# Gathered cumulative sum and matmul on one core: rows converted to fp16 by the gather's own transfer, with 32 slots paced by landings, in place of fp32 slots and a ScalarE cast

## The chip, the core and the metric

The kernel runs on one core of a Trainium2 chip. The metric is the device time of one execution in microseconds. A core has TensorE (PE, matmuls; its weight loads are shown apart as PEld), VectorE (DVE), ScalarE (ACT), GpSimd (POOL), SyncE (SP), and 16 DMA engines that all queues share. Each engine works through its own list of instructions in order; engines wait for one another by semaphores.

## The reference

```python
B, S, N, D = (16, 4096, 2048, 512)          # x: (B, S, D) float32, w: (D, D) float32
# indices: (B, N) int64, per batch N different rows out of S, sorted
gathered = x[b_idx, indices, :].copy()
cs = np.cumsum(gathered, axis=1)
return np.matmul(cs, w).astype(np.float32)   # (B, N, D)
```

For each of 16 batches, 2048 rows of 512 numbers are picked out, summed cumulatively along the rows, and multiplied by w.

## The kernel before

The work is cut into T = 256 tiles of P = 128 gathered rows, 16 tiles (NT) to a batch; two tiles (R) make a pair. A tile passes through these steps, each on one engine:

1. POOL, `gather` (L127, the transfer at L137): an indirect DMA brings 128 rows of x, 2 KB each, into half of a buffer `g32` (8 buffers of a pair, so NG = 16 slots of a tile, fp32). Each slot has a semaphore `s_g` that the landing raises. Before a pair is gathered into a used buffer, POOL waits (L130) until the casts that read it are done (`s_c`).
2. ACT, `cast` (L148, L152): waits for landings and copies `g32` into `g16` (8 buffers of a pair, fp16), a tile or a whole pair at once.
3. PE, `sums` (L156, L164): four matmuls of 128 columns multiply the tile with a triangle of ones (`ut`), which gives the running sums within the tile, transposed, in the PSUM buffer `pa` (4 of them). Its columns are ordered so that two adjacent output rows come to one partition. PE waits for the cast (L159), for a free `pa`, and for a free `pb` of the coming projection (L163).
4. DVE, `carry` (L173, L196): adds the last column of the tile before, and writes `cst` as fp16. The first tile of a batch is only copied (L183).
5. PE, `project` (L200, L208): four matmuls of 512 columns multiply by w (fp16) into the PSUM buffer `pb` (4 of them).
6. ACT, `drain` (L217, L220): copies `pb` into an output buffer `ob` (8 buffers of a pair, fp32).
7. SP, `store` (L222, L234): when a pair is drained, a DMA of 512 KB writes it out. The first and the last pair, which use the triangle `uq` with rows in plain order, are stored tile by tile (L229).

The order of the work is written out by hand for each engine. On PE, a list `order` puts the sums of up to `lead` tiles ahead of projection u: `lead` is 1 at the start, grows with u to LEAD = 4, and shrinks to 1 at the end. On ACT, step u first waits, at every second tile, for the buffer `ob` to be stored, then makes the casts of step u, then drains tile u. How far those casts reach is planned at L114 to L122: two tiles ahead of u at the start, one more for each four tiles, FAR = 10 at most, and fewer again at the end; from a reach of five on they are made in pairs. PE, DVE and ACT have the first and last tiles unrolled, and roll the middle in loops of 16 tiles (U).

At the start, indices of the first four tiles come through two small loads (`idx_first`), and POOL gathers those tiles at once; the others come through `idx64`, a conversion to fp32, a transpose on PE and a copy back to integers (`idxg`), for which the gather of tile 4 waits. w is loaded as fp32 and cast half by ACT and half by DVE.

Of the kernel before, what the change touches and what calls it, by code (L numbers as in the profile page):

```python
# [7 lines left out]
P = 128  # L8
FP32 = mybir.dt.float32
FP16 = mybir.dt.float16  # L10
# [23 lines left out]
def kernel(  # L34
# [7 lines left out]
    nc = tc.nc  # L42

    B, S, D = x.shape
    N = indices.shape[1]
    R = 2
# [3 lines left out]
    T = B * NT  # L50
    G = T // R
    GB = NT // R
    KI = T // P
    FIRST = 2 * R
    NG = 16
    LEAD = 4
    FAR = 10
    NH = 8
    NA = 4
    NB = 4  # L60
    NC = 4
    NO = 8
    U = NT
    assert U % NG == 0 and U % (R * NO) == 0 and U % NA == 0 and U % (R * NC) == 0 and U % NB == 0
    assert D == 512 and N % (R * P) == 0 and T % P == 0

    x_flat = x.rearrange("b s d -> (b s) d")
# [1 line left out]
    const = ctx.enter_context(tc.tile_pool(name="const", bufs=1))  # L69
# [10 lines left out]
    ident = const.tile([P, P], FP32)  # L80
    zeros = const.tile([P, D], FP16)
    spare = const.tile([P, 1], FP16)
    g32 = [const.tile([P, R, D], FP32, name=f"g32_{i}") for i in range(NG // R)]
    g16 = [const.tile([P, R, D], FP16, name=f"g16_{i}") for i in range(NH)]
    cst = [const.tile([P, DC, R, P], FP16, name=f"cst{i}") for i in range(NC)]
    ob = [const.tile([P, R, D], FP32, name=f"ob{i}") for i in range(NO)]
    pa = [ps.tile([P, DC, R, Q], FP32, name=f"pa{i}") for i in range(NA)]
    pb = [ps.tile([P, D], FP32, name=f"pb{i}") for i in range(NB)]

# [2 lines left out]
    def sem(name):  # L92
        return tc.alloc_semaphore(name)

    s_z, s_ut, s_wc, s_if, s_pt, s_prep, s_of, s_c = (
        sem(f"s_{n}") for n in ("z", "ut", "wc", "if", "pt", "prep", "of", "c")
    )
    s_first = [sem(f"s_first{k}") for k in range(2)]
    s_w = [sem(f"s_w{c}") for c in range(DC)]
    s_idx = [sem(f"s_idx{k}") for k in range(KI)]  # L100
    s_el = [sem(f"s_el{j}") for j in range(R)]
    s_ol = [sem(f"s_ol{j}") for j in range(R)]
    s_g = [sem(f"s_g{i}") for i in range(NG)]
    s_o = [sem(f"s_o{i}") for i in range(NO)]
    s_a = sem("s_a")
    s_d = sem("s_d")
    s_b = sem("s_b")
    s_e = sem("s_e")

    pool, pe, dve, act, sp = (  # L110
        Lane(e) for e in (nc.gpsimd, nc.tensor, nc.vector, nc.scalar, nc.sync)
    )

    casts = []  # L114
    cast_by = []
    for u in range(T):
        far = min(FAR, 2 + u // 4, 2 + (T - 1 - u) // 4)
        casts.append([])
        while len(cast_by) <= min(u + far, T - 1):
            n = R if far > 4 and len(cast_by) % R == 0 else 1  # L120
            casts[u].append((len(cast_by), n))
            cast_by += [cast_by[-1] + 1 if cast_by else 1] * n  # L122

    for u in range(3 * U, T - 2 * U):
        assert casts[u] == [(t + U, n) for t, n in casts[u - U]]

    def gather(t):  # L127
        g, r = divmod(t, R)
        if t >= NG:
            pool.need(s_c, cast_by[R * (g + 1) - NG - 1])  # L130
        if t < FIRST:
            pool.need(s_first[g], 16)
            ap = idx_first[:, t, 0:1]
        else:
            pool.need(s_prep, t // P + 1)
            ap = idxg[:, t // P, t % P : t % P + 1]
        nc.gpsimd.indirect_dma_start(  # L137
            out=g32[g % (NG // R)][:, r, :],
            out_offset=None,
            in_=x_flat,  # L140
            in_offset=bass.IndirectOffsetOnAxis(ap=ap, axis=0),
            element_offset=(t // NT) * S * D,
        ).then_inc(s_g[t % NG], 16)
# [1 line left out]

    PLAIN = (0, G - 1)

    def cast(t, n, first=None):  # L148
        g, r = divmod(t, R)
        for u in range(t, t + n):  # L150
            act.need(s_g[u % NG], 16 * (u // NG + 1), first)
        nc.scalar.copy(  # L152
            out=g16[g % NH][:, r : r + n], in_=g32[g % (NG // R)][:, r : r + n]
        ).then_inc(s_c, 1)

    def sums(t, u, first=None):  # L156
        g, r = divmod(t, R)
        tiles = None if first is None else R * first
        pe.need(s_c, cast_by[t] if first is None else cast_by[2 * U + t] - 2 * U // R, first)  # L159
        pe.need(s_d, t - NA + 1, tiles)  # L160
        for c in range(DC):
            if c == 1 and u is not None:
                pe.need(s_e, u - NB + 1, tiles)  # L163
            mm = nc.tensor.matmul(  # L164
                out=pa[t % NA][:, c],
                lhsT=g16[g % NH][:, r, c * P : (c + 1) * P],
                rhs=uq[:] if first is None and g in PLAIN else ut[:],
                start=(c == 0),
                stop=(c == DC - 1),
            )  # L170
        mm.then_inc(s_a, 1)
# [28 lines left out]
    def project(u, t, first=None):  # L200
        g, j = divmod(u, R)
        tiles = None if first is None else R * first
        pe.need(s_e, u - NB + 1, tiles)
        pe.need(s_d, u + 1 if first is None and g in PLAIN else R * (g + 1), tiles)
        for c in range(DC):
            if c == 2 and t is not None:
                pe.need(s_d, t - NA + 1, tiles)
            mm = nc.tensor.matmul(  # L208
                out=pb[u % NB][:],
                lhsT=cst[g % NC][:, c, j, :],  # L210
                rhs=w16[:, c, :],
                start=(c == 0),
                stop=(c == DC - 1),
            )
        mm.then_inc(s_b, 1)

    def drain(u, first=None):  # L217
        g, j = divmod(u, R)
        act.need(s_b, u + 1, first)
        nc.scalar.copy(out=ob[g % NO][:, j], in_=pb[u % NB][:]).then_inc(s_e, 1)  # L220

    def store(g):  # L222
        b, h = divmod(g, GB)
        rows = out[b, h * R * P : (h + 1) * R * P, :]
        if g in PLAIN:
            for j in range(R):
                sp.need(s_e, R * g + j + 1)
                done = s_ol[j] if g else (s_o[0], s_of)[j]
                nc.sync.dma_start(  # L229
                    out=rows[j * P : (j + 1) * P, :], in_=ob[g % NO][:, j]  # L230
                ).then_inc(done, 16)
            return
        sp.need(s_e, R * (g + 1))
        nc.sync.dma_start(  # L234
            out=rows.rearrange("(p j) d -> p j d", j=R), in_=ob[g % NO][:]
        ).then_inc(s_o[g % NO], 16)


    with nc.allow_non_contiguous_dma(reason="a few indices, one per partition"):
        for k, eng in enumerate((nc.sync, nc.scalar)):  # L240
            t = k * R
            eng.dma_start(
                out=idx_first[:, t : t + R, :],
                in_=indices[0, t * P : (t + R) * P]
# [4 lines left out]
    for k in range(KI):  # L249
        nc.sync.dma_start(  # L250
            out=idx64[:, k, :], in_=idx_rows[k * P : (k + 1) * P, :]
        ).then_inc(s_idx[k], 16)
    for c in range(DC):
        eng = (nc.sync, nc.scalar)[c % 2]
        eng.dma_start(out=w32[:, c, :], in_=w[c * P : (c + 1) * P, :]).then_inc(s_w[c], 16)
    for g in range(G):
        store(g)
    for g in range(G - NO, G - 1):
        sp.need(s_o[g % NO], 16 * (g // NO + 1))
    for j in range(R):  # L260
        sp.need(s_ol[j], 16)


    nc.gpsimd.memset(ident[:], 1.0).then_inc(s_ut, 1)
# [3 lines left out]
        out=ident[:],  # L268
        in_=ident[:],
# [7 lines left out]
        out=ut[:],  # L277
        in_=ut[:],
# [9 lines left out]
        out=uq[:],  # L288
        in_=uq[:],
# [6 lines left out]
    for t in range(T):  # L296
        gather(t)
# [15 lines left out]
    for k in range(KI):  # L313
# [3 lines left out]
            out=pb[k % NB][:, :P], in_=idxf[:, k, :], identity=ident[:]  # L317
# [20 lines left out]
    order = []  # L338
    done = 0
    for u in range(T):  # L340
        lead = min(LEAD, 1 + (u + 2) // 4, 1 + (T - 1 - u) // 6)
        first = u if u // R in PLAIN else u // R * R + R - 1
# [2 lines left out]
            done += 1  # L345
        order.append((False, u))

    head = order.index((False, 2 * U - 1)) + 1
    tail = order.index((False, T - 2 * U - 1)) + 1
    step = 2 * U  # L350
    for i in range(head + step, tail):
        assert order[i] == (order[i - step][0], order[i - step][1] + U)

    def run(i, first=None):
        is_sums, t = order[i]
        after = next((v for k, v in order[i + 1 :] if k != is_sums), None)
        if first is not None:
            t -= 2 * U
            after -= 2 * U
        if is_sums:  # L360
            sums(t, after, first)
        else:
            pe.need(s_wc, DC)
            project(t, after, first)

    for i in range(head):
        run(i)
    with nc.tensor.Fori(2 * U // R, (T - 2 * U) // R, U // R) as first:
        pe.new_pass()
        for i in range(head, head + step):  # L370
            run(i, first)
    for i in range(tail, len(order)):
        run(i)
# [5 lines left out]
        act.need(s_w[c], 16)  # L379
        nc.scalar.copy(out=w16[:, c, :], in_=w32[:, c, :]).then_inc(s_wc, 1)  # L380
    def step(u, first=None):
        if u % R == 0:
            if first is None and u == R * NO:
                act.need(s_of, 16)
            act.need(s_o[u // R % NO], 16 * (u // R // NO), first)
        for t, n in casts[u if first is None else 2 * U + u]:
            cast(t if first is None else t - 2 * U, n, first)
        drain(u, first)


    for u in range(2 * U):
        step(u)
# [36 lines left out]
```

## Time and profile before

| what | value |
|---|---|
| time, median of 4 runs (lowest to highest) | 353.01 us (352.86 to 354.24) |
| the profiled execution: its own time | 352.79 us |
| its span, first to last instruction | 351.1 us |
| mean TensorE clock granted | 0.985 |
| busy: PE, PEld, DVE, ACT, POOL | 306.1, 156.2, 179.2, 262.5, 244.4 us |
| moved by DMA | 135.69 MB, mean 386 GB/s |
| HBM read, written | 68.42 MB, 67.11 MB |
| issue to landing, median: gather, store of 512 KB, store of 256 KB | 10.1, 6.7, 3.8 us |

In the prediction, lines of costly groups read: line of the kernel, engine, operation, output from input, count; then busy time in total and mean ns of one; then the idle time of the engine just before these instructions and what ended most of it ("issue" is time in which the engine waited for nothing that the profile shows). A strip has 40 numbers, one for each equal slice of the span. A queue's line gives its packets, its megabytes and the time that its packets took as a share of the 16 DMA engines' span; q0 carries the gathers and q1 nearly all else. A line of the chain of waits has the start and the duration in us, the engine and the line of the kernel. Landing times give the shortest, the median and the longest from issue to landing.

### The profile page before, as it was taken

The page shows a single profiled execution, that of the slowest core. Times are in us where ns is not written, and L with a number is a line of the kernel's source. Part 1 is how long each engine was busy: PE and PEld are TensorE (multiplying, and loading weights), DVE is VectorE, ACT ScalarE, POOL GpSimd, SP SyncE. Part 2 cuts the span into 40 slices and gives each one's busy share as a digit, 9 for nine tenths or more (in the row PEclk, how much of TensorE's full clock was granted, in tenths as well). Part 3 has the DMA queues.
Part 4 walks back from the last instruction along what each step waited for, and adds up shares of the span by engine and source line. Part 5 has one row for each costly group of instructions (what it writes and reads, how often), then busy time and mean ns, then how long its engine had stood idle before and what let it go on. Part 6 is the DMA issues. An engine that isn't in the chain of part 4 may idle for free.

```text
span 351.1 us, 6498 instructions
## 1 busy us (share of the span) xinstructions
PE 306.1 (87%) x2066; PEld 156.2 (44%) x2066; DVE 179.2 (51%) x263; ACT 262.5 (75%) x399; POOL 244.4 (70%) x266
## 2 busy tenths in 40 slices
PE   7656799989998989989898988989898999899993
PEld 2323355444444444444444444445444444445541
DVE  2433356555555555545555554555555555556451
ACT  3555599687787878778787877777787877788872
POOL 6777777777777777777777777777777777776000
PEclk9998899999999999999999999999999999999998
DMA  7899999999999999999999999999999999999983
GB/s 232 245 331 315 300 350 411 414 411 416 413 415 414 416 416 414 416 414 414 414 414 414 413 412 409 410 413 411 414 409 404 413 408 413 412 411 412 418 338 140
DMA packets 40619, 135.69 MB, mean 386 GB/s; under 512 B 6816, under 2 KB 7072, under 8 KB 40608
## 3 DMA queue, kind: packets, MB, share of 16 engines
q0 software_dynamic: 20480, 67.13, 50.0%
q1 hardware_dynamic: 19568, 67.91, 48.0%
q10 hardware_dynamic: 560, 0.53, 0.4%
q8 instruction: 5, 0.08, 0.1%
q14 instruction: 6, 0.05, 0.0%
HBM read 68.42 MB, written 67.11 MB: 386 GB/s over the span
## 4 chain that ended last, share of the span: by engine, by line
POOL 43%; DMA 18%; issue 16%; PE 15%; ACT 6%; DVE 0%; ACTq 0%; SPq 0%
POOL g L137 43%; DMA g<-in_x_dram,idxg 16%; PE pb L208 11%; ACT g L152 4%; PE pa L164 3%; ACT ob L220 2%; DMA g<-in_x_dram,idx_first 1%; DMA idx_first<-in_indices_dram 1%; DVE cst L183 0%; DVE cst L196 0%; ACTq L26 0%; ACTq L393 0%; SPq L424 0%; SPq L90 0%
## 5 line engine op out<-in xcount | busy, mean ns | idle before, releaser
L137 POOL DMA_INDIRECT g<-in_x_dram,idxg x252 | 238.9, 948 | 76.8 <-issue 71.4
L208 PE MATMUL pb<-w,cst 128*128 128x512 f16 x1024 | 264.8, 382 | 1.0 <-DVE cst L196 0.8
L196 DVE TENSOR_TENSOR cst<-pa,cst 128x512 f16<-128x512 f32 x240 | 166.1, 692 | 144.8 <-PE pa L164 143.9
L152 ACT CAST g<-g 128x1024 f16<-128x1024 f32 (+1 forms) x139 | 135.9, 979 | 58.2 <-DMA g<-in_x_dram,idxg 57.3
L220 ACT COPY ob<-pb 128x512 f32<-128x512 f32 x256 | 138.5, 586 | 19.6 <-PE pb L208 19.5
L164 PE MATMUL pa<-ut,g 128*128 128x128 f16 x1008 | 113.7, 222 | 34.9 <-ACT ob L220 22.2
L164 PEld LDWEIGHTS pa<-ut,g 128*128 128x128 f16 x1008 | 73.4, 98 | 116.3 <-ACT ob L220 53.8
L208 PEld LDWEIGHTS pb<-w,cst 128*128 128x128 f16 x1024 | 90.1, 98 | 64.1 <-issue 2.6
L183 DVE CAST cst<-pa 128x512 f16<-128x512 f32 x16 | 11.1, 692 | 13.3 <-PE pa L164 13.3
L304 PE MATMUL pb<-zeros 128*128 128x512 f16 x16 | 5.7, 524 | 1.5 <-DVE zeros L308 1.5
L137 POOL DMA_INDIRECT g<-in_x_dram,idx_first x4 | 4.0, 997 | 1.6 <-issue 0.9
L304 PEld LDWEIGHTS pb<-zeros 128*128 128x128 f16 x16 | 2.0, 132 | 4.0 <-issue 1.9
L380 ACT CAST w<-w 128x512 f16<-128x512 f32 x2 | 1.1, 616 | 3.0 <-DMA w<-in_w_dram 3.0
L377 ACT ACT_TABLE_LOAD x1 | 1.3, 1283 | 2.5 <-issue 2.5
L164 PE MATMUL pa<-uq,g 128*128 128x128 f16 x16 | 1.6, 220 | 1.7 <-ACT g L152 1.7
L311 DVE CAST idxf<-idx 128x128 f32<-128x128 uint32 x2 | 0.5, 227 | 4.1 <-DMA idx<-in_indices_dram 4.1
L164 PEld LDWEIGHTS pa<-uq,g 128*128 128x128 f16 x16 | 1.0, 97 | 3.0 <-issue 1.7
L325 DVE CAST w<-w 128x512 f16<-128x512 f32 x2 | 0.8, 424 | 1.3 <-DMA w<-in_w_dram 1.3
L316 PE MATMUL pb<-ident,idxf 128*128 128x128 f32 x2 | 0.9, 448 | 0.3 <-DVE idxf L311 0.3
L316 PEld LDWEIGHTS pb<-ident,idxf 128*128 128x128 f32 x2 | 0.4, 182 | 1.2 <-DVE idxf L311 0.8
L308 DVE MEMSET zeros<- 128x256 uint32 x1 | 0.3, 272 | 1.1 <-SPq L90 1.1
L322 DVE CAST idxg<-pb 128x128 uint32<-128x128 f32 x2 | 0.6, 288 | 0.4 <-PE pb L316 0.4
(11 smaller groups left out, 2.1 us busy)
## 6 DMA issues: line engine op xcount, KB each, us to landing
out_dram<-ob SPq DMA_DIRECT2D x126, 512.0 KB, 6.7
g<-in_x_dram,idxg POOLq DMA_INDIRECT x252, 10.1
out_dram<-ob SPq DMA_DIRECT2D x4, 256.0 KB, 3.8
w<-in_w_dram ACTq DMA_DIRECT2D x2, 256.0 KB, 4.1
w<-in_w_dram SPq DMA_DIRECT2D x2, 256.0 KB, 4.8
idx<-in_indices_dram SPq DMA_DIRECT2D x2, 128.0 KB, 3.4
g<-in_x_dram,idx_first POOLq DMA_INDIRECT x4, 4.6
idx_first<-in_indices_dram ACTq DMA_DIRECT2D x1, 2.0 KB, 2.1
```

The lines of the kernel that those rows point to most:

```text
L137: nc.gpsimd.indirect_dma_start(out=g32[g % (NG // R)][:, r, :], out_offset=None, in_=x_flat, in_offset=bass.IndirectOffsetOnAxis(ap=ap, ax ...
L152: nc.scalar.copy(out=g16[g % NH][:, r : r + n], in_=g32[g % (NG // R)][:, r : r + n]).then_inc(s_c, 1)
L164: mm = nc.tensor.matmul(out=pa[t % NA][:, c], lhsT=g16[g % NH][:, r, c * P : (c + 1) * P], rhs=uq[:] if first is None and g in PLAIN else ...
L183: nc.vector.tensor_copy(out=dst, in_=src).then_inc(s_d, 1)
L196: nc.vector.tensor_tensor(out=dst, in0=src, in1=last, op=mybir.AluOpType.add).then_inc(s_d, 1)
L208: mm = nc.tensor.matmul(out=pb[u % NB][:], lhsT=cst[g % NC][:, c, j, :], rhs=w16[:, c, :], start=(c == 0), stop=(c == DC - 1),)
L220: nc.scalar.copy(out=ob[g % NO][:, j], in_=pb[u % NB][:]).then_inc(s_e, 1)
L304: nc.tensor.matmul(out=pb[NB - 1][:], lhsT=zeros[:, :P], rhs=zeros[:], start=True, stop=True)
L316: nc.tensor.transpose(out=pb[k % NB][:, :P], in_=idxf[:, k, :], identity=ident[:]).then_inc(s_pt, 1)
L325: nc.vector.tensor_copy(out=w16[:, c, :], in_=w32[:, c, :]).then_inc(s_wc, 1)
L377: nc.scalar.copy(out=spare[:], in_=zeros[:, :1])
L380: nc.scalar.copy(out=w16[:, c, :], in_=w32[:, c, :]).then_inc(s_wc, 1)
```

## The change

- The gather (L125 after the change) writes into fp16 buffers `g16` at once: 16 buffers of a pair, 32 slots of a tile (NG). The DMA converts fp32 to fp16 on its way. `g32` and ScalarE's cast, with its plan of casts, are removed.
- POOL's waits are others. Ahead of the first gather of a pair, it waits until the sums of the tiles that used the two slots before are done (`s_a`, the pair 32 tiles back). Ahead of the second, from tile 17 on, it waits for the landing of the gather 16 tiles before (FLY), so that at most 17 gathers are on their way.
- PE's sums wait for the landing (`s_g`) in place of the cast.
- Output buffers hold two pairs (W = 2) and there are four of them, as much room as before; a store of 1 MB writes two pairs. The first two pairs and the last two are stored singly, the very first and last still tile by tile. ACT waits for a free output buffer at every fourth tile.
- PE's loop has 32 tiles (V) in its body in place of 16. ACT's loop keeps 16 tiles and has drains and waits for output buffers alone.

Cut to its core:

```diff
-    NG = 16
+    NG = 32
+    FLY = 16
     LEAD = 4
-    FAR = 10
-    NH = 8
...
-    NO = 8
+    W = 2
+    NO = 4
     U = NT
+    V = 2 * U
...
-    g32 = [const.tile([P, R, D], FP32, name=f"g32_{i}") for i in range(NG // R)]
-    g16 = [const.tile([P, R, D], FP16, name=f"g16_{i}") for i in range(NH)]
+    g16 = [const.tile([P, R, D], FP16, name=f"g16_{i}") for i in range(NG // R)]
...
-    ob = [const.tile([P, R, D], FP32, name=f"ob{i}") for i in range(NO)]
+    ob = [const.tile([P, W, R, D], FP32, name=f"ob{i}") for i in range(NO)]
...
     def gather(t):
         g, r = divmod(t, R)
-        if t >= NG:
-            pool.need(s_c, cast_by[R * (g + 1) - NG - 1])
+        if r == 0:
+            pool.need(s_a, R * (g + 1) - NG)
+        elif t >= FLY:
+            pool.need(s_g[(t - FLY) % NG], 16 * ((t - FLY) // NG + 1))
...
         nc.gpsimd.indirect_dma_start(
-            out=g32[g % (NG // R)][:, r, :],
+            out=g16[g % (NG // R)][:, r, :],
...
-    def cast(t, n, first=None):
-        g, r = divmod(t, R)
-        for u in range(t, t + n):
-            act.need(s_g[u % NG], 16 * (u // NG + 1), first)
-        nc.scalar.copy(
-            out=g16[g % NH][:, r : r + n], in_=g32[g % (NG // R)][:, r : r + n]
-        ).then_inc(s_c, 1)
-
     def sums(t, u, first=None):
...
-        pe.need(s_c, cast_by[t] if first is None else cast_by[2 * U + t] - 2 * U // R, first)
+        pe.need(s_g[t % NG], 16 * (t // NG + 1), first)
...
-        nc.scalar.copy(out=ob[g % NO][:, j], in_=pb[u % NB][:]).then_inc(s_e, 1)
+        nc.scalar.copy(out=ob[g // W % NO][:, g % W, j], in_=pb[u % NB][:]).then_inc(s_e, 1)
...
-        sp.need(s_e, R * (g + 1))
+        sp.need(s_e, R * (g + n))
+        done = {1: s_of, G - W: s_ol}.get(g, s_o[g // W % NO])
         nc.sync.dma_start(
-            out=rows.rearrange("(p j) d -> p j d", j=R), in_=ob[g % NO][:]
-        ).then_inc(s_o[g % NO], 16)
+            out=rows.rearrange("(g p j) d -> p g j d", p=P, j=R),
+            in_=src[:, g % W : g % W + n],
+        ).then_inc(done, 16)
...
-    for g in range(G):
-        store(g)
...
+    for g in range(W):
+        store(g, 1)
+    for g in range(W, G - W, W):
+        store(g, W)
+    for g in range(G - W, G):
+        store(g, 1)
...
-    with nc.tensor.Fori(2 * U // R, (T - 2 * U) // R, U // R) as first:
+    with nc.tensor.Fori(V // R, (T - V) // R, V // R) as first:
...
     def step(u, first=None):
-        if u % R == 0:
-            if first is None and u == R * NO:
-                act.need(s_of, 16)
-            act.need(s_o[u // R % NO], 16 * (u // R // NO), first)
-        for t, n in casts[u if first is None else 2 * U + u]:
-            cast(t if first is None else t - 2 * U, n, first)
+        if u % (W * R) == 0:
+            if first is None and u == W * R * NO:
+                act.need(s_of, 16 * (R + W - 2))
+            act.need(s_o[u // R // W % NO], 16 * (u // R // W // NO), first)
         drain(u, first)
```

More of the change, by code (lines that the diff above doesn't have):

```diff
@@ L61 @@
     NC = 4
-    NO = 8
+    W = 2
+    NO = 4
     U = NT
-    assert U % NG == 0 and U % (R * NO) == 0 and U % NA == 0 and U % (R * NC) == 0 and U % NB == 0
+    V = 2 * U
+    assert V % NG == 0 and V // R == 16 and U % (W * R * NO) == 0 and U % NA == 0 and U % (R * NC) == 0 and U % NB == 0
     assert D == 512 and N % (R * P) == 0 and T % P == 0
@@ L100 @@
     s_idx = [sem(f"s_idx{k}") for k in range(KI)]
-    s_el = [sem(f"s_el{j}") for j in range(R)]
-    s_ol = [sem(f"s_ol{j}") for j in range(R)]
+    s_ol = sem("s_ol")
     s_g = [sem(f"s_g{i}") for i in range(NG)]
@@ L112 @@
     )
[L114 to L125, printed above, removed]
     def gather(t):
         g, r = divmod(t, R)
-        if t >= NG:
-            pool.need(s_c, cast_by[R * (g + 1) - NG - 1])
+        if r == 0:
+            pool.need(s_a, R * (g + 1) - NG)
+        elif t >= FLY:
+            pool.need(s_g[(t - FLY) % NG], 16 * ((t - FLY) // NG + 1))
         if t < FIRST:
@@ L165, in sums @@
                 out=pa[t % NA][:, c],
-                lhsT=g16[g % NH][:, r, c * P : (c + 1) * P],
+                lhsT=g16[g % (NG // R)][:, r, c * P : (c + 1) * P],
                 rhs=uq[:] if first is None and g in PLAIN else ut[:],
@@ L219, in drain, with store @@
         act.need(s_b, u + 1, first)
-        nc.scalar.copy(out=ob[g % NO][:, j], in_=pb[u % NB][:]).then_inc(s_e, 1)
-    def store(g):
+        nc.scalar.copy(out=ob[g // W % NO][:, g % W, j], in_=pb[u % NB][:]).then_inc(s_e, 1)
+    def store(g, n):
         b, h = divmod(g, GB)
-        rows = out[b, h * R * P : (h + 1) * R * P, :]
+        rows = out[b, h * R * P : (h + n) * R * P, :]
+        src = ob[g // W % NO]
         if g in PLAIN:
@@ L227, in store @@
                 sp.need(s_e, R * g + j + 1)
-                done = s_ol[j] if g else (s_o[0], s_of)[j]
+                done = s_ol if g else (s_o[0], s_of)[j]
                 nc.sync.dma_start(
-                    out=rows[j * P : (j + 1) * P, :], in_=ob[g % NO][:, j]
+                    out=rows[j * P : (j + 1) * P, :], in_=src[:, g % W, j]
                 ).then_inc(done, 16)
             return
-        sp.need(s_e, R * (g + 1))
+        sp.need(s_e, R * (g + n))
+        done = {1: s_of, G - W: s_ol}.get(g, s_o[g // W % NO])
         nc.sync.dma_start(
-            out=rows.rearrange("(p j) d -> p j d", j=R), in_=ob[g % NO][:]
-        ).then_inc(s_o[g % NO], 16)
+            out=rows.rearrange("(g p j) d -> p g j d", p=P, j=R),
+            in_=src[:, g % W : g % W + n],
+        ).then_inc(done, 16)
     with nc.allow_non_contiguous_dma(reason="a few indices, one per partition"):
@@ L255 @@
         eng.dma_start(out=w32[:, c, :], in_=w[c * P : (c + 1) * P, :]).then_inc(s_w[c], 16)
-    for g in range(G):
-        store(g)
[L258 to L261, printed above, removed]
+    for g in range(W):
[4 more added lines that the diff above has]
+        store(g, 1)
+    for i in range(G // W - NO, G // W - 1):
+        sp.need(s_o[i % NO], 16 * (i // NO + 1))
+    sp.need(s_ol, 16 * (R + W - 1))
     nc.gpsimd.memset(ident[:], 1.0).then_inc(s_ut, 1)
@@ L346 @@
         order.append((False, u))
-    head = order.index((False, 2 * U - 1)) + 1
-    tail = order.index((False, T - 2 * U - 1)) + 1
-    step = 2 * U
+    head = order.index((False, V - 1)) + 1
+    tail = order.index((False, T - V - 1)) + 1
+    step = 2 * V
     for i in range(head + step, tail):
-        assert order[i] == (order[i - step][0], order[i - step][1] + U)
+        assert order[i] == (order[i - step][0], order[i - step][1] + V)
     def run(i, first=None):
@@ L357, in run @@
         if first is not None:
-            t -= 2 * U
-            after -= 2 * U
+            t -= V
+            after -= V
         if is_sums:
```

## The prediction

> **What bounds the kernel now.** I read the page's costliest groups first, then the rate strip, the waits, and last the landings and the chain by stage.
>
> ```profile
> span 351.1 us, 6498 instructions
> L137 POOL DMA_INDIRECT g<-in_x_dram,idxg x252 | 238.9, 948 | 76.8 <-issue 71.4
> L208 PE MATMUL pb<-w,cst 128*128 128x512 f16 x1024 | 264.8, 382 | 1.0 <-DVE cst L196 0.8
> L152 ACT CAST g<-g 128x1024 f16<-128x1024 f32 (+1 forms) x139 | 135.9, 979 | 58.2 <-DMA g<-in_x_dram,idxg 57.3
> ```
>
> A gather keeps POOL 0.948 us and the next follows 0.30 us later, so one every 1.253 us. The timeline of POOL shows the first of these 252 at 8.39 us and the last at 322.89: 314.5/251 = 1.253. The gap is 0.30 both for gathers with no wait (tiles 4 to 15) and for those whose wait on a cast has been met. POOL is thus never held up, and its last gather can't go out before 322.9.
>
> ```profile
> GB/s 232 245 331 315 300 350 411 414 411 416 413 415 414 416 416 414 416 414 414 414 414 414 413 412 409 410 413 411 414 409 404 413 408 413 412 411 412 418 338 140
> q0 software_dynamic: 20480, 67.13, 50.0%
> q1 hardware_dynamic: 19568, 67.91, 48.0%
> ```
>
> A slice is 8.78 us. From slice 7 the transfers run flat at about 414 GB/s: a second bound. A tile is 262,144 B gathered and 262,144 B stored; at 414 GB/s that is 0.633 + 0.633 = 1.266 us, just over POOL's 1.253. All 135.69 MB at 414 would take 327.8 us. The first six slices fall short of 414 by 182+169+83+99+114+64 = 711 GB/s, or 711 x 8.78/414 = 15.1 us of this rate; the last two by 350, or 7.4 us. 327.8 + 15.1 + 7.4 = 350.3, the span. The head's 15.1 us is what can be won: why are the stores late there? The chain of waits from 16 to 24 us shows it:
>
> ```profile
> 17.49 0.59 ACT ob L220
> 18.08 0.53 ACT g L152
> 18.61 0.05 issue
> 18.65 0.40 PE pa L164 x4
> 19.05 0.88 PE pb L208 x4
> 19.93 0.02 issue
> 19.95 0.59 ACT ob L220
> ```
>
> Drain, cast, sums, project, drain: 2.46 us for a tile, twice the gather's pace. ACT's program has the cast of tile u+2 or u+3 ahead of drain u and behind drain u-1; the sums of that tile stand ahead of projection u on PE. So no two stages overlap. By 45 us only 19 tiles are drained, while 33 are gathered. Later ACT must cast up to tile u+10 before it drains u, so outputs stay some 10 tiles behind landings. The time from issue to landing of the gathers, for 20 to 45 us, 45 to 60 us and 300 to 325 us:
>
> ```profile
> DMA to landing us min/median/max: 4.3/5.2/7.0
> ```
> ```profile
> DMA to landing us min/median/max: 6.6/7.4/7.7
> ```
> ```profile
> DMA to landing us min/median/max: 14.7/15.7/16.5
> ```
>
> The last gather, issued at 322.89, lands at about 339.4. Behind it stands a fixed tail: the sums of tile 255 start at 343.06, the last drain at 345.39, the span ends at 351.1; 8.04 us from sums to end.
>
> **What the Trainium skill says.** "DMA: Bandwidth & Descriptors", section "SWDGE vs HWDGE vs iDMA", allows a cast during a DMA only on GpSimd's transfers; it gives no price, and no transfer of this trace converts. The same page's "Where 436 GB/s comes from" puts the ceiling at 435 GB/s; the trace's 414 agrees that transfers are near full. Its "Queues, rings and completion order" says that an engine alternates between queues packet by packet; the two queues' shares of 50.0% and 48.0% for nearly equal bytes fit that. "Collectives: The Full Stack", "The bandwidth ceiling: the fold count and why AG ≠ RS ≠ AR", says that the inline add costs no rate of its own, only the second read does. A conversion is another inline operation, so this is a hint and no price.
>
> **The change part by part.**
>
> *ScalarE's 139 casts go* (135.9 us of ACT). In the middle ACT had waits of 57.3 us on landings, so the busy time itself is worth nothing there. Two things on the path go. In the head, the chain of 2.46 us opens: PE waits for the landing itself, projection u stands only behind the sums of at most tile u+4, and drains wait for PE alone. PE's own pace is 0.22 + 0.86 = 1.09 us a tile (chain, 310 to 340 us), below 1.253, so outputs follow the gathers. Tile 11 is then drained when tile 15 has landed (22.2 + 5.0) and two more us have passed, near 29 us. By then some 18 gathers (4.7 MB), 1.3 MB of indices and weights and 12 tiles stored (3.1 MB) are through: 9.1 of the 12.0 MB that 414 GB/s would move, a loss of 2.9 MB or 7.0 us in place of 15.1. In the tail, landing to sums shrinks from 343.06 - 339.4 = 3.7 us to about 0.1.
>
> *The gather converts.* It still reads 2 KB a row and writes 1 KB. Its price isn't in the trace. Ends: by written bytes it would be 0.317 us of transfer a tile, half of 0.633; if reading, converting and writing did not overlap, twice, 1.266. I take 0.633, the read side unchanged, which is the nearest row. POOL's 0.948 us too may change[...]: from -0.05 us (128 rows to address are left, so little can go) to +0.2 us (an estimate, a fifth of 0.948); I take 0.
>
> *Waits at the gather.* The first of a pair now waits for the sums 30 tiles back, 30 x 1.253 = 37.6 us, against a landing of about 10 us and a lag of 5 tiles: met long before. The second waits for the landing 16 back, issued 20.0 us before, against at most 16.5 us. Met too, and a met wait fits in the 0.30 us gap. If landings exceeded 20 us it would bind; behind it on POOL stand only gathers, for which PE would wait.
>
> *Stores of two pairs.* 64 issues in place of 126 on SP, which holds nothing else then. The first pair of two waits 2 tiles longer (2.5 us), hidden while gathers fill the transfers; the last two pairs still go alone. Landing of 1 MB lies between 6.7 us (the row of 512 KB) and 13.4. ACT reuses a buffer after 12 other tiles, 15.0 us: a cover of 1.6 us at the worst end; uncovered, drains would slip by the excess once in four tiles.
>
> *PE's loop body of 32 tiles in place of 16*: 6 passes in place of 12, the same matmuls. Taken as nothing; the instruction queues carry 0.1% now.
>
> *The sum.* Last gather issued at 322.89, as before. Its landing: about 235 tiles from 29 us on, each 1.266 - 1.253 = 0.013 us short, gives 3.1 us of backlog. The same account tests on before: landings grew by 15.7 - 7.4 = 8.3 us in 211 gathers, one landing per 1.292 us or 203 GB/s; stores had the other 211, so they caught up 8 tiles x 0.633 = 5.1 us, and 3.2 us remains for the shortage. Without a lag to catch up, 5.2 to 7.4 us grows to 8.3 to 10.5; I take 9. Landed at 331.9, + 0.1 + 8.04 = 340.0. By bytes: 327.8 + 7.0 + 6 (tail idle) = 340.8, in agreement. The profiled execution took 352.79 us, 1.69 over its span, and stands 0.22 below the median of 353.01. 340.0 + 1.7 = **341.7 us**. What is late next: POOL's issue and the transfers, at equal pace.
>
> **The rivals.**
>
> *Cheaper transfers* (same side): at 0.317 + 0.633 = 0.95 us a tile no backlog forms, and landings stay at 4.7 us. 322.89 + 4.7 + 0.1 + 8.04 + 1.7 = 337.4 us. For it: half the bytes reach SBUF. Against: the read is as long.
>
> *Dearer converting transfers* (slower): the row's conversion lengthens the time its packet holds an engine. The transfers are saturated, so each per cent is 252 x 0.00633 = 1.6 us; from (352.8 - 341.7)/1.6 = 7% on it is slower than before. At 25%, 0.158 us a tile, the gather waits for landings (1.424 us a tile): 341.7 + 39.9 = 381.6 us. Twice the time would give 502. For it: no slack in the transfers, and no converting row anywhere in the trace. Against: only the skill's hint on inline operations.
>
> *Dearer issue on POOL* (slower): the first 0.013 us is hidden, then 252 x each excess; from about 0.057 us on slower. At 0.1 us, 341.7 + 252 x 0.087 = 363.6, less the backlog of 3.1 that can't form: 360.5 us.
>
> *The head's gain does not come*: another order limits outputs there (projections in wait of landings two to five tiles on, stores held for two pairs), and only the tail's 3.7 us is won, less 1 for larger stores: about 350 us.
>
> **How the numbers follow.** Equal transfer 0.40, cheaper 0.19, no gain in the head 0.06, dearer transfer 0.27, dearer issue 0.08. A measurement of this kernel can tell about 0.3%, 1.1 us, from no change. Faster: 0.40 + 0.19 + most of 0.06 and a little of the dearer cases below 7% = 0.64; within: 0.04; slower: 0.32. The range starts at 335, the cheaper case with landings at 3.7 us and a tail 1 us shorter. At the top it reaches into both dear cases: 375, a transfer 21% dearer or an issue 0.16 us longer, which leaves about 0.18 above it and 0.02 below. Of the faster cases alone the range is 335 to 350.
>
> **What would show it.** Right: gathers still every 1.253 us from 8.4 to 322.9; the rate strip near full from its fourth slice; ACT's drains from 12 us on at about 1.25 us a tile; landings of 8 to 11 us at the end; no time put down to the wait for landings on POOL. (With a strip that counts written bytes, look at the share of DMA instead.) Wrong: q0's share of the engines well off half; landings near 20 us with POOL waiting on DMA, which is the dearer transfer; a DMA_INDIRECT well over 0.95 us, the dearer issue; landings of 4 to 5 us throughout, the cheaper one.

## The result, and the profile after

The changed kernel takes 354.8 us (median of 35 runs, 353.97 to 356.92) beside 353.19 us for the kernel before (56 runs): 1.0053 of it, 95% interval 1.0042 to 1.0063. It is 0.5% slower, where 3% faster was forecast. Its profiled execution took 354.93 us, with a span of 353.2. Some of the experiments below ran on chips on which the kernel before took 445 to 453 us, and are compared with that alone. Ratios are taken between the fast runs of both kernels, so they can differ a little from the quotient of the medians of all runs.

The page after: the span, the gather, the projection, the rate strip and the two large queues, in the order shown of before.

```profile
span 353.2 us, 6041 instructions
L125 POOL DMA_INDIRECT g<-in_x_dram,idxg x252 | 237.1, 941 | 78.5 <-issue 64.3
L188 PE MATMUL pb<-w,cst 128*128 128x512 f16 x1024 | 264.0, 381 | 0.8 <-DVE cst L176 0.8
...
GB/s 191 156 177 289 273 312 288 288 309 289 303 307 297 295 310 295 293 319 285 301 312 294 299 305 300 291 308 304 291 302 303 302 294 309 300 290 319 302 336 227
...
q0 software_dynamic: 36864, 33.57, 58.7%
q1 hardware_dynamic: 18576, 67.90, 50.2%
HBM read 68.42 MB, written 67.11 MB: 384 GB/s over the span
```

POOL is as before: 0.941 us and 0.30, the last gather at 322.75. The strip counts a gather by its written bytes, so it is flat near 300 where before it was flat near 414; the bytes at HBM are those of before. The gathers' queue is what moved: half the megabytes, but 36,864 packets in place of 20,480 (144 a gather in place of 80), and its packets now hold the engines for 58.7% in place of 50.0%, while the stores' queue stays near its share. (The two add up to more than 100%: packets of the two queues overlap, so these shares are a sign of the cost and not its size.)

The landings of the gathers after, again for 20 to 45, 45 to 60 and 300 to 325 us:

```profile
DMA to landing us min/median/max: 3.7/6.6/8.2
```
```profile
DMA to landing us min/median/max: 7.6/8.3/9.1
```
```profile
DMA to landing us min/median/max: 20.0/21.0/22.3
```

The time to land grows by 12.7 us (8.3 to 21.0), half as much again as the 8.3 before (7.4 to 15.7), and the last gather lands at 345.1. The waits after show who is held:

```profile
ACT ob L200 <- PE pb L188: 190.4, 256, 3.6
...
PEld pa L144 <- DMA g<-in_x_dram,idxg: 90.3, 110, 2.5
...
PE pa L144 <- DMA g<-in_x_dram,idxg: 40.9, 69, 2.0
...
POOL g L125 <- DMA g<-in_x_dram,idxg: 5.1, 11, 0.6
```

PE now waits for landings all along, and POOL only at the end, when they pass 20 us. These are the signs that the prediction had named for the dearer transfer: q0's share well off half, landings near 20 us, POOL waiting on DMA. The chain of drain, cast, sums and projection is gone: the chain of waits from 16 to 26 us holds nothing but POOL's issue, and the drains from 10 to 45 us are busy for 13.3 us in place of 9.4, at 0.586 us each 23 tiles in place of 16. (The 19 of the prediction counted drains twice that a window's edge cuts.)

### The profile page after: what moved, and what is told of

Read it like the earlier page. It is cut to its first block, busy times and chain, and to the rows that moved or that the text cites. A ratio compares the mean times of both kernels' runs of the same rounds, so it can differ in the third digit from the quotient of the medians.

```text
span 353.2 us, 6041 instructions
## 1 busy us (share of the span) xinstructions
PE 303.2 (86%) x2066; PEld 152.4 (43%) x2066; DVE 179.5 (51%) x263; ACT 152.7 (43%) x260; POOL 242.6 (69%) x266
## 3 DMA queue, kind: packets, MB, share of 16 engines
q0 software_dynamic: 36864, 33.57, 58.7%
## 4 chain that ended last, share of the span: by engine, by line
DMA 51%; POOL 28%; issue 10%; PE 9%; DVE 0%; ACT 0%; SPq 0%
DMA g<-in_x_dram,idxg 50%; POOL g L125 28%; PE pb L188 6%; PE pa L144 3%; DMA idx_first<-in_indices_dram 1%; DVE cst L176 0%; ACT ob L200 0%; SPq L408 0%; SPq L90 0%
## 5 line engine op out<-in xcount | busy, mean ns | idle before, releaser
L125 POOL DMA_INDIRECT g<-in_x_dram,idxg x252 | 237.1, 941 | 78.5 <-issue 64.3
L200 ACT COPY ob<-pb 128x512 f32<-128x512 f32 x256 | 150.1, 586 | 190.4 <-PE pb L188 190.4
L144 PE MATMUL pa<-ut,g 128*128 128x128 f16 x1008 | 98.6, 220 | 41.6 <-DMA g<-in_x_dram,idxg 40.9
L144 PEld LDWEIGHTS pa<-ut,g 128*128 128x128 f16 x1008 | 69.6, 98 | 124.3 <-DMA g<-in_x_dram,idxg 90.3
L163 DVE CAST cst<-pa 128x512 f16<-128x512 f32 x16 | 11.1, 691 | 6.1 <-PE pa L144 6.1
L125 POOL DMA_INDIRECT g<-in_x_dram,idx_first x4 | 4.0, 989 | 1.6 <-issue 0.9
```

The source lines that it names most:

```text
L125: nc.gpsimd.indirect_dma_start(out=g16[g % (NG // R)][:, r, :], out_offset=None, in_=x_flat, in_offset=bass.IndirectOffsetOnAxis(ap=ap, ax ...
L144: mm = nc.tensor.matmul(out=pa[t % NA][:, c], lhsT=g16[g % (NG // R)][:, r, c * P : (c + 1) * P], rhs=uq[:] if first is None and g in PLAI ...
L163: nc.vector.tensor_copy(out=dst, in_=src).then_inc(s_d, 1)
L200: nc.scalar.copy(out=ob[g // W % NO][:, g % W, j], in_=pb[u % NB][:]).then_inc(s_e, 1)
```

## The experiments

Theory A: the converting gather costs transfer time, and the rest of the change brings what was forecast. Rival B: conversion is free, and pacing, store size or PE's waits for landings eat the gain. Kernels whose labels begin with the same letter ran on the same chip, and ratios are to the kernel before on it. It took 445 to 453 us beside e, f and i, whose own chains are for the most part PE; 452 us beside g, whose kernels hold little but transfers and ran them at the full rate; and 353 to 354 us beside h and s.

**The whole change without its conversion** (e1, f1, h1).

```diff
-    ut = const.tile([P, R, Q], FP16)
-    uq = const.tile([P, P], FP16)
+    ut = const.tile([P, R, Q], BF16)
+    uq = const.tile([P, P], BF16)
...
-    g16 = [const.tile([P, R, D], FP16, name=f"g16_{i}") for i in range(NG // R)]
+    g32 = [const.tile([P, R, D], FP32, name=f"g32_{i}") for i in range(NG // R)]
...
-                lhsT=g16[g % (NG // R)][:, r, c * P : (c + 1) * P],
+                lhsT=g32[g % (NG // R)][:, r, :].bitcast(BF16)[:, 2 * c * P + 1 : 2 * (c + 1) * P : 2],
```

> The kernel after, but the gather brings plain fp32 rows into 32 slots of 2 KB, and PE takes the upper two bytes of each number as bf16 for its weights (so the inputs are cut to bf16; nothing converts). Theory A (the converting transfer costs 7% more of transfer time, about 0.044 us a tile, and everything else of the change brought what was forecast): 341 to 344 us, landings of 8 to 11 us at the end. Rival B (a conversion costs no transfer time; pacing by landings, larger stores or PE's waits for landings eat the gain): 352 to 356 us.

> The same kernel as e1_plain_gather (the kernel after with plain fp32 gathers into 32 slots, PE taking the upper two bytes of each number as bf16), again, since the chip of that run took 445 us for the kernel before. Theory A (the dearer converting transfer alone lost the gain): 341 to 344 us, landings of 8 to 11 us at the end. Rival B (pacing, larger stores or waits for landings eat the gain): 352 to 356 us.

> The same kernel as e1_plain_gather and f1_plain_gather, on a further chip. Transfers alone gave 0.060 us for the conversion of a tile. Theory A (the rest of the change brings what was forecast): after's 354.8 less 256 x 0.060 = 15.4, so 339 to 343 us where before takes 353. Rival B (another part of the change holds the time too, and takes over as the limit): 347 to 353 us.

e1 took 422.7 us, 0.9515 (0.9463 to 0.9568) of before's 445.4; f1 421.7, 0.950 (0.9419 to 0.9582). They don't bear on the question, as the kernel after this one (e4) shows. h1 took 348.59 us, 0.9877 (0.9856 to 0.9897) of 352.98: between the two expectations. Against after's 1.0053, the conversion costs 1.76% of before, 6.2 us; the rest of the change gains 4.4 us, not the forecast 11.3. Both theories hold a part. PE's times don't differ by its bf16 weights: a matmul of the sums took 221 ns beside 220. The page of h1, its strip and queue, and its landings for 300 to 325 us:

```profile
span 346.4 us, 6041 instructions
...
GB/s 226 265 301 380 354 404 383 418 411 415 414 416 415 416 418 414 418 416 414 413 413 416 412 415 414 408 416 415 414 414 413 413 414 416 413 413 415 411 317 193
...
q0 software_dynamic: 20480, 67.13, 49.9%
```
```profile
DMA to landing us min/median/max: 13.5/14.1/14.8
```

With slices of 8.66 us, the first eight fall short of 414 by 188+149+113+34+60+10+31-4 = 581, or 12.2 us; the last two by 318, or 6.7 us. 327.8 + 12.2 + 6.7 = 346.7, close to its span of 346.4. The head lost 12.2 us where the forecast had 7.0.

**Half the gathered bytes** (e4): h1's kernel with rows of 1 KB, each of 256 numbers used twice, so that half of the input is left out. Cut to its core:

```diff
-    x_flat = x.rearrange("b s d -> (b s) d")
+    x_flat = x.rearrange("b s (k d) -> (b s k) d", k=2)
```

> As e1_plain_gather, but a gathered row is 1 KB (256 of the numbers, each used twice, so half of the input is left out): as many bytes written to a slot as after the change, nothing converted, half read. If the price of a transfer follows its bytes, the transfers have slack, POOL's issue alone is the limit, landings stay at 4 to 5 us, and the time is 336 to 339 us. If small rows as such are dear (by row, not by byte), landings grow past 10 us and the time is over 345 us.

421.6 us beside e1's 422.7, on the same chip: 33.6 MB less to move changed 1.1 us. On that chip the transfers were not the limit, and none of the kernels e, f and i, which all compute, can tell what a transfer costs. Inconclusive for the question.

**The conversion alone in the kernel before** (e2, f2): ScalarE copies fp16 to fp16.

```diff
-    g32 = [const.tile([P, R, D], FP32, name=f"g32_{i}") for i in range(NG // R)]
+    g32 = [const.tile([P, R, D], FP16, name=f"g32_{i}") for i in range(NG // R)]
```

> The kernel before, with one edit: the 16 slots are fp16, so that the gather converts, and ScalarE copies fp16 to fp16 at the same places. Theory A (dearer converting transfer): before is at the transfers' limit too, so some 256 x 0.03 to 0.044 us are added, 360 to 365 us, and q0 holds near 58% of the engines. Rival B (free conversion): 351 to 354 us.

> The same kernel as e2_before_convert (before with fp16 slots, a converting gather and ScalarE copying fp16 to fp16), again. Theory A: 256 x 0.03 to 0.044 us dearer, 360 to 365 us. Rival B: 351 to 354 us.

449.3 us, 1.0107 (1.0031 to 1.0184), and 448.3, 1.006 (1.0024 to 1.0095). Dearer both times, but on chips limited otherwise, so the size says nothing.

**The head's chain alone in the kernel before** (e3, f3, i2).

```diff
-        far = min(FAR, 2 + u // 4, 2 + (T - 1 - u) // 4)
+        far = min(FAR, 3 + u // 3, 2 + (T - 1 - u) // 4)
```

> The kernel before, with one edit: in the head the casts reach one tile further ahead and grow faster (3 + u // 3 in place of 2 + u // 4), so that the cast that projection u needs is no longer behind drain u-1. Theory A (the head's chain of drain, cast, sums and projection costs transfer time that can be won): 345 to 350 us, 25 or more tiles drained by 45 us in place of 19. Rival B (the head's loss can't be won, since the transfers' total sets the end): 352 to 354 us.

> The same kernel as e3_before_far (before, its first casts reaching one tile further ahead and growing faster), again. Theory A (transfer time lost in the head can be won): 345 to 350 us. Rival B: 352 to 354 us.

> The same kernel as e3_before_far (before, its first casts reaching one tile further ahead and growing faster), on a further chip. Theory A (the head's chain of drain, cast, sums and projection costs transfer time that can be won): 345 to 350 us, 25 or more tiles drained by 45 us in place of 19. Rival B (the head's room is lost in another way as soon as the chain is open): 351 to 354 us.

444.7, 443.2 and 449.2 us: 0.9962 (0.9927 to 0.9998), 0.9918 (0.9849 to 0.9987), 0.9925 (0.990 to 0.9951). A gain of 0.4 to 0.8% each time, on such chips again; what it is worth where before takes 353 us was not measured.

**Rows over 4096 B a pair** (f4): h1's kernel with rows of 528 numbers, cut otherwise out of x, so other numbers are summed. Cut to its core:

```diff
-    x_flat = x.rearrange("b s d -> (b s) d")
+    L = 528
+    rows = B * S * D // L
+    x_flat = x.rearrange("b s d -> (b s) d")[: rows * L].rearrange("(n e) -> n e", e=L)
```

> As f1_plain_gather, but a gathered row has 528 numbers, 2112 B, in place of 2048 (rows cut otherwise out of x, so other numbers are summed): two rows are over 4096 B. A converting gather went out as 144 packets (nine per DMA engine, one row each and one at the end), a plain one as 80 (two rows each). Theory P (the price of a conversion is that of single-row packets, four more per engine and tile, 0.044 us in all): 144 packets a gather, plain; 0.044 us for packets and 3.1% of 0.633, 0.020 us, for bytes: a tile every 1.33 us, 13 to 16 us more than f1_plain_gather. Rival C (the conversion itself costs, packets don't): only the bytes count, 3 to 6 us more than f1_plain_gather.

421.35 us: inconclusive, like f1 beside it.

**Transfers alone, with 5 stores for 16 gathers** (g1 to g4). No sums, carries, projection or drains; SP stores zeros. Its program, condensed:

```python
for i in range(T // NT * 5):
    t = i // 5 * NT + 3 * (i % 5 + 1)
    sp.need(s_g[t % NG], 16 * (t // NG + 1))    # landing of gather t
    if i >= NO:
        sp.need(s_o[i % NO], 16 * (i // NO))    # NO = 4 on their way
    store(i)                                    # 1 MB of zeros
```

> Transfers alone: the 256 gathers of plain fp32 rows into 32 slots, each waiting for the landing 16 before, and 5 stores of 1 MB of zeros for every 16 gathers (80 in all, in place of 64), each behind the landing of a gather; sums, carries, projection and drains are left out. The stores' excess makes the transfers the limit: by 0.633 us for 262,144 B, 16 gathers and 5 stores take 22.8 us, all 365 us, and with start and end 375 to 390 us. It is the base of the three beside it; the theories do not differ on it.

> As g1_dma_plain, but the gather converts to fp16. Theory A (a converting gather takes 0.044 us more of all the transfers' time): 256 x 0.044 = 11 us over g1_dma_plain. Rival B (conversion is free, and after lost its time elsewhere): within 2 us of it, or below it by up to 80 us if written bytes were what counts.

> As g1_dma_plain, but plain rows of 528 numbers, 2112 B, so that two rows are over 4096 B. Theory P (the price of a conversion is that of packets of one row): 144 packets a gather as when converting; 11 us for packets and 256 x 0.020 = 5 us for bytes, 16 us over g1_dma_plain. Rival C (the conversion itself costs): 5 us over it.

> As g3_dma_528, but rows of 496 numbers, 1984 B, two of which fit into 4096 B: the control for rows that begin at no multiple of 2048 B. Theory P: 80 packets a gather, 256 x 0.020 = 5 us below g1_dma_plain. If where a row begins is what costs in g3_dma_528, it is above g1_dma_plain here too.

376.59, 391.97, 381.61 and 372.31 us, each with all its runs within 0.9 us. The strip of g1 is flat from its fifth slice to its last but one, so the transfers are the limit; below it, what g1 and g2 moved at HBM:

```profile
GB/s 119 308 375 408 417 419 419 419 419 420 419 418 420 418 418 419 419 418 419 418 418 418 418 419 418 419 419 419 418 420 419 418 419 419 419 418 418 419 422 261
```
```profile
HBM read 67.38 MB, written 83.89 MB: 403 GB/s over the span
```
```profile
HBM read 67.38 MB, written 83.89 MB: 387 GB/s over the span
```

 The conversion costs 15.4 us, 15.4/256 = 0.060 us a gather, 9.5% of 0.633. g3 lies 5.0 us above g1 and g4 4.3 below; by bytes at 419 GB/s it would be 5.0 each way (256 x 128 rows x 64 B). So where a row begins costs nothing that these runs can tell. The gathers' queue in g1, g2, g3 and g4:

```profile
q0 software_dynamic: 20480, 67.13, 44.8%
```
```profile
q0 software_dynamic: 36864, 33.57, 52.3%
```
```profile
q0 software_dynamic: 20480, 69.22, 45.7%
```
```profile
q0 software_dynamic: 16384, 65.03, 43.8%
```

Theory P failed in its premise: the longer plain rows went out in 80 packets as well, so no plain run had packets of one row. But g4's went out in 64, one fewer per DMA engine and gather, and it gained nothing beyond its bytes. If a packet more cost the 0.060/4 = 0.015 us that P now needs, one fewer would have given 3.8 us. That speaks against packets and for the conversion itself; it isn't settled.

**Store size undone in the kernel after** (i1).

```diff
-    W = 2
-    NO = 4
+    W = 1
+    NO = 8
...
-        done = {1: s_of, G - W: s_ol}.get(g, s_o[g // W % NO])
+        done = s_o[g % NO]
```

> The kernel after with one part undone: output buffers and stores of one pair (512 KB, 8 buffers) as before; conversion, slots, pacing and loops as after. Theory S (stores of two pairs leave later in the head, where the transfers have room, and this room is lost; it is what kept the plain version at 348.6 where 341.7 was forecast): 2 to 4 us below after, 351 to 353 us. Rival L (the head's room is lost through the order on PE and the pace of landings, not the size of stores): within 1 us of after, 354 to 356 us.

426.4 us, 0.9412 (0.9338 to 0.9487) of 453.3: inconclusive for the stores, since the kernel after was not timed on that chip and transfers were not its limit.

**The transfers of the kernel after alone, at their real number** (s1 to s3). As g, but 64 MB of stores in the kernel's own order:

```python
u = R * (g + n) - 1                             # last tile of the store
t = min(T - 1, u + min(LEAD, 1 + (u + 2) // 4, 1 + (T - 1 - u) // 6))
sp.need(s_g[t % NG], 16 * (t // NG + 1))
```

> The transfers of the kernel after at their real number, alone: 256 plain gathers, POOL's waits as after (landings for the slots in place of sums), 64 MB stored as after (pairs singly at both ends, 1 MB otherwise), each store behind the landing of the gather that PE's order puts ahead of the last tile in it; sums, carries, projection and drains are left out, so stores leave 2 to 3 us earlier than in h1_plain_gather and the tail is some 4 us shorter. From h1_plain_gather's 348.6: 341 to 345 us by either theory, if the head's loss is one of transfers and their order alone; 336 to 339 us if the loss came from compute.

> As s1_skeleton_double with stores of one pair (512 KB, 8 on their way). Theory S (stores of two pairs leave late in the head): 2 to 4 us below s1_skeleton_double. Rival L (order and landings, not the size of stores): within 1 us of it.

> As s1_skeleton_double with converting gathers. With 5 stores for 16 gathers a conversion cost 0.060 us a tile; all of it exposed is 15 us. Theory A' (where the transfers are not full, in head and tail, the dearer gather is hidden, as after against h1_plain_gather, 6.2 us, suggests): 5 to 9 us over s1_skeleton_double. Rival (all of it shows, and after is helped by something else): 13 to 16 us over it.

341.68, 341.93 and 352.76 us. Store size changes nothing: theory S fell. The conversion costs 11.1 us here, between the two expectations. The strip of s1, which has hardly an engine at work but POOL and the queues, and its landings for 300 to 325 us:

```profile
span 340.0 us, 465 instructions
...
GB/s 107 279 320 350 377 381 390 419 418 416 418 418 418 417 418 418 417 418 418 418 419 418 418 415 418 418 418 420 416 418 417 418 418 417 419 417 418 419 418 250
```
```profile
DMA to landing us min/median/max: 8.9/9.4/10.5
```

The first seven slices of 8.5 us fall short of 418 by 722, or 14.7 us. This kernel doesn't load w; its 1.05 MB would fill 2.5 us of it (an estimate), which leaves 12.2 us, as much as h1 lost. Nothing but POOL's pace and the order "a store behind the landing of a later gather" is at work here, so the loss in the head comes with this order, without any compute. Stored singly (s2), its first seven slices lose 13.3 us in place of 14.7, and yet the time is the same: room won in the head does not come back one for one.

## Why the prediction was wrong

The likeliest case gave 341.7 us and faster; the range of 335 to 375 held the time, the direction was wrong. The difference of 13.1 us splits by runs: 348.6 - 341.7 = 6.9 us is missing without any conversion, and the conversion brings the other 6.2.

*The converting gather: the step that failed.* "I take 0.633, the read side unchanged" was mis-sized: where transfers are the limit, the conversion added 0.060 us, which makes it 0.693 (g1, g2). All that the prediction had against a dearer transfer, the hint of an inline add at no rate of its own, did not carry over to a conversion. The rival of dearer transfers had it, and the measured 9.5% lies past its turning point of 7%. But that point stood on a gain of 11 us elsewhere, and its price for 9.5%, 15.2 us, is what g showed; in the kernel itself the conversion cost 6.2 us, and the kernel became slower only because the rest had gained no more than 4.4.

*A count that lags: not in the prediction.* A gather raises its semaphore by 16 in single counts, and what waits for its landing waits for all of them. The trace has the time of each. Medians of the time in us from issue to the eighth, the fifteenth and the last count, for gathers of 45 to 60 us and, behind the arrow, of 300 to 325 us (gathers with all 16 counts in the trace):

| kernel | 8th count | 15th count | 16th count, the landing |
|---|---|---|---|
| before | 5.7 → 6.2 | 7.2 → 7.4 | 7.4 → 15.7 |
| h1, plain | 6.0 → 6.3 | 6.8 → 8.4 | 7.1 → 14.1 |
| s1, plain transfers alone | 6.1 → 7.1 | 7.2 → 9.1 | 7.4 → 9.4 |
| after | 5.8 → 17.0 | 6.6 → 18.5 | 8.3 → 21.0 |
| s3, converting transfers alone | 6.0 → 17.8 | 6.5 → 19.5 | 7.0 → 19.9 |

In before and in h1, what grows is one count of 16; by its number presumably that of one of the 16 DMA engines, though the trace doesn't name it. With the conversion all of them fall behind. That is the plainest sign that the conversion made the transfers as a whole dearer. The table also tells why it shows as 11.1 us in the transfers alone and as 6.2 in the kernel. The fifteenth count of the last gather comes 11.3 us later in after than in h1 (342.4 beside 331.1), much as in s3 beside s1 (343.4 beside 332.4). But h1 then waits 5.8 us more for the last count and after only 2.7, and from the last landing to the end h1 takes 1.4 us longer: 11.3 - 3.1 - 1.4 = 6.8 us, the difference of the two spans. What slows the one count, and why less in after, is open. In s1 it is 0.5 us late at the end, in s2 2.1, so most of it comes with what the transfers alone leave out.

*The backlog at the end: 9 us taken, 14.1 found without conversion* (h1, 300 to 325 us). The working had split the growth of 8.3 us in before into a shortage of the rate and a catching up of the stores. By the table it was neither, but the one count: the fifteenth grew by 0.2 us, so that but for this one count the transfers of before kept up with POOL's 1.253 us. Nor do stores run ahead. Between 60 and 310 us before moved 52.28 MB of gathers and 50.89 MB on the stores' queue, and h1 and s1 moved these:

```profile
q0 software_dynamic: 15985, 52.41, 52.4%
q1 hardware_dynamic: 13272, 51.18, 50.2%
```
```profile
q0 software_dynamic: 16002, 52.45, 51.8%
q1 hardware_dynamic: 13490, 51.98, 50.8%
```

In h1 the fifteenth count of the last gather comes at 331.1, where the forecast had the landing at 331.9; the sixteenth comes at 336.9. These 5.0 us, 1.4 more from landing to end, and 0.5 more between span and time are the 6.9 us that are missing without conversion.

*The head: mis-sized.* The chain opened as forecast, 23 tiles drained by 45 us (22 in h1) where before drained 16, but the loss fell from 15.1 to 12.2 us (h1), not to 7.0. The working counted 12 tiles as stored when the last of them was only drained: tiles 8 to 11, 1.05 MB or 2.5 us, had still to move. It also took the transfers as full from 29 us on; h1's strip stays below 414 until its eighth slice, past 60 us. Counted by bytes, opening the chain was worth about 3 us, not 8. This is another way to count the same time, and not to be added to the 6.9 us above. Whether a smaller loss in the head would have ended h1 sooner isn't shown: s1 loses as much there, and its last gather lands at 332.8 all the same.

*Luck.* That s1 takes 341.68 us beside the forecast's 341.7 proves nothing for the working. It doesn't load w (2.5 us), runs at 418 and not 414 GB/s (3.1 us over its bytes) and ends sooner, its last slice short by 3.4 us where 6 were taken; together this makes up for the 7.7 us that its head loses over the forecast's 7.0.

*Right.* POOL's pace and its waits: a met wait fits the 0.30 us gap (30 waits on sums, 9.1 us in all), and the landing wait bound only as landings passed 20 us, 5.1 us in all. POOL's issue of a converting gather: 0.941 us beside 0.948, inside the given -0.05 to +0.2. Stores of two pairs: nothing lost by s1 and s2, and landing in 8.0 us in after, between the given 6.7 and 13.4. PE's loop of 32 tiles: PE's waits for issue come to 1.1 us at most in a row of sums or projections. The tail: from the sums of tile 255 at 345.35 to the end at 353.2 are 7.85 us, forecast 8.04; from landing, at 345.1, to sums is 0.3 us, forecast 0.1. These right terms could not save a sum whose largest unknown, the price of the conversion, was set to zero.

## What to carry to other kernels

Where transfers run at their limit, a conversion done by the gather is no free cast: it halved the bytes written, not the time, and here added 0.060 us to 0.633 us of transfer. An engine relieved of 136 us of work gives nothing back unless its waits ended the path; the head's chain looked like 8 us and was worth 3 by bytes, since transfers alone in the same order are as short of full. To know which, run the transfers alone in the kernel's own order: these kernels settled here what most runs of whole kernels had left open. And a landing is the last of its 16 counts: before a growing time to land is read as a full transfer queue, see whether all the counts grow or one.

## What the runs showed of the hardware that was not expected

- A converting gather of 128 rows of 2 KB goes out as 144 packets, a plain one as 80; plain rows of 2112 B as 80, of 1984 B as 64, of 1 KB (e4) as 48. Each time 16 of them hold 4 B. The others hold 4096 B in before (two rows), 4224 B in g3 (two), 5952 or 3968 B in g4 (three and two) and 4096 B in e4 (four); converting, 1024 B written (one row). So plain rows were put together until 4096 B were reached, converting ones not at all.
- In before and h1 the time to land grew by 8.3 and 7.0 us while the fifteenth of a gather's 16 counts came only 0.2 and 1.6 us later: one count set the landing. Its cause was not found.
- POOL's issue of a gather took 0.981 us with rows of 1984 B, 0.944 with 2112 B, and 0.945 with 2048 B and with 1 KB.
- On some chips the kernel before took 445 to 453 us. The TensorE clock granted to it there was 0.87 to 0.92, beside 0.97 to 1.00 where it took 353. In e1's trace PE is 70% of the chain that ended last, and DVE and ACT wait up to 16 and 20 us on releases that the trace can't name; transfers alone ran at 419 GB/s on such a chip all the same. There the changed kernel's structure gained 5% without its conversion (e1, f1) and 6% with it and single stores (i1), where without it it gained 1.2% on the chip of h1. So what the structure gains depends on the chip; why was not followed up.
- The fastest whole kernel found, h1 at 348.6 us, reads every second 2-byte half of fp32 numbers as PE's weights (its inputs are so cut to bf16): a weight load took 98 ns as with fp16 side by side, so the step of 4 bytes cost nothing.
